# A hybrid decoder layer on one core: 18 output products of the second token tile move behind the last attention head, and the first feed-forward block is computed one token tile at a time

## The chip, the core and the metric

The kernel runs on one core of a Trainium2 chip. The metric is the device time of one execution in microseconds (us). The core has five engines that run their own instruction queues and meet only at semaphores: PE (TensorE, the matrix products; its weight loads are shown apart as PEld), DVE (VectorE), ACT (ScalarE), POOL (GpSimd) and SP, whose queue issues most of the DMAs here.

## The reference, cut to what matters

One layer on 256 tokens of width 1024, float32. `x` is projected; two groups of 8 heads (latent attention and block-sparse attention, which on 256 tokens is plain causal attention with a distance penalty) give `concat(A, B)` of width 1024. Then:

```
x = layer_norm(alpha * x + concat(A, B) @ W_o)
h = causal_depthwise_conv3(x @ W_up)          # 2 * 2816 columns
x = layer_norm(alpha * x + (silu(gate) * up) @ W_down)
```

The tolerance of float32 is reached by splitting each factor of a product into a rounded part (`hi`, float32r) and a remainder (`lo`): a product is hi x hi, hi x lo and lo x hi. TensorE takes a float32r product in one record; a plain float32 product (the scores and values of the heads) shows as two.

## The kernel before, in words

Tokens lie in two tiles of 128 (t = 0, 1), the model width in eight blocks of 128 (k = 0 to 7), the feed-forward width in 22 blocks (f = 0 to 21), each with a gate half (w = 0) and an up half (w = 1).

**Attention.** 16 heads run one behind the other: `scores` (PE), softmax (DVE and ACT), `transposes` (PE), `values` (PE). Between these steps the PE is given independent products out of the list `todo`, in pieces of so many moving rows as `FILL` says: 1500 after the scores, 1500 after the values, 1700 after the transposes. The list holds first the projections that later heads need and then the output products `wo` of block k and token tile t (`gen_wo`, 3 products for each of two groups of 512 columns). One product counts its moving columns, and a piece ends with the product that reaches the number. In this stage the PE's products are kept in the order of the program.

**Output products behind the last head.** What is left of the list runs, then, in this order: two runs of `late` (k = 4 and 5 of tile 1, first column group, 3 products each), the 6 products of (k = 7, t = 0), which end tile 0, and the six other runs of `late` (first column group of k = 6 and 7, then the second group of k = 4 to 7). The sums lie in PSUM tiles `pm`.

**First layer norm and turning.** Each step of it is pinned (`pin`, `tc.keep_in_program_order`), so that every engine takes these steps in the order of the program. Tile 0: add to the residual (L494), statistics (L500), aggregate (L505), root on ACT (L506), then the add of tile 1's first column group (L494), reciprocal (L511), shift (L515), scale on ACT (L528). PE turns tile 0 in two tiles of four 128x128 transposes, `a0` (k 0 to 3) and `a4` (k 4 to 7). Gain and offset (`affine`, L551 on ACT, L553 on DVE) write `x1T`; `high` (L557, ACT) writes `x1hi`, `low` (L560, POOL or DVE) writes `x1lo`. Tile 1 follows with four tiles of two transposes. `keep_warm` (L101) puts five idle products between.

```
ln_root(0, 0)
ln_add(0, 1, 0, r1, x_sb[:, 1, :], pm)
mu, rs, nm = ln_scale(0, 0)
ln_shift(mu, rs, nm)
```

**Feed-forward.** `up(f, w)` multiplies a block of `W_up` with `x1` (both token tiles): for f = 0 (and the very last half block) by 24 products of 256 columns (L611, L612, L615); for the others by 8 products of 512 columns (hi with x1hi and x1lo side by side, L621) and 8 of 256 (lo with x1hi, L624), whose two halves are then added by an ACT copy `hb` (L626) and a DVE add `h` (L628). These products are not pinned; the planner puts them where its own model finds room.

**Weights.** A block of weights is loaded into `raw`, cast to `hi` on ACT (L87), and `lo` is the difference on DVE (L88). Each of the three has 7 buffers. A block's `hi` and `lo` are free again when its last product is done. From f = 1 on, the splits of the up half and of f = 2 wait for the last steps of turning (`late_split`).

Of the kernel before, what the change touches and what calls it, by code (L numbers as in the profile page):

```python
# [33 lines left out]
TURN_AFTER = 4  # L34
LAG = 2
BEFORE = 2
A0, A4 = 2, 0
WARM = (6, 5)
WARM_NARROW = 3
HELD = 6  # L40
HALVES = ((0, 512), (512, 512))
COLS = ((HALVES, HALVES), (HALVES, ((0, 512), (512, 256), (768, 256))))
ATTW_BUFS = 2
FILL = (8000, 1500, 1500, 1700)
EARLY = 1
NARROW = 1
RES = 8
RAW_BUFS, HI_BUFS, LO_BUFS = 7, 7, 7

# [2 lines left out]
def layer_kernel(ctx: ExitStack, tc: tile.TileContext, a, out):  # L52
# [371 lines left out]
    todo = [("q1", gen_q(1), 0)] + [(f"va{t}", gen_va(t), 0) for t in range(NT)] + [("k2", gen_k(2), 0)]  # L424
    todo += [(f"q{pr}", gen_q(pr), 0) for pr in (2, 3)]
    todo += [(f"qk{w}{pr}", gen_qk(w, pr), 0) for pr in range(NP) for w in range(2)][EARLY:]
    todo += [(f"wo{k}{t}", gen_wo(k, t), 2 * k + 2) for k in range(NP) for t in range(NT)]
    todo += [(f"wo{k}0", gen_wo(k, 0), 2 * k + 2) for k in range(NP, KT - 1)]
    done = set()
    over = 0  # L430

# [18 lines left out]
    def run(gen):  # L450
        for _ in gen:
            pass
# [24 lines left out]
    x_sb = att_pool.tile([P, NT, D], F32, tag="m8b", name="x_sb")  # L477
    for t in range(NT):
        nc.gpsimd.dma_start(x_sb[:, t, :], a["x"][:, t, :])
    late = [(k, 1, (grp,)) for grp in COLS[0][1] for k in range(NP, KT)]  # L480
    for k, t, cols in late[:2] + [(KT - 1, 0, None)] + late[2:]:
        run(gen_wo(k, t, cols))

    r = acts.tile([P, NT, D], F32, tag="r", name="r")
    x1 = acts.tile([P, KT, 2, S], F32R, tag="x", name="x1")
# [5 lines left out]
    def ln_add(i, t, j, dst, res, acc):  # L491
        o, n = COLS[i][t][j]
        sl = slice(o, o + n)
        pin(nc.vector.scalar_tensor_tensor(dst[:, sl], res[:, sl], ALPHA, acc[t, o][:, :n], op0=ALU.mult, op1=ALU.add))  # L494

    def ln_part(i, t, j, src):
        w = min(n for _, n in COLS[i][t])
        o, n = COLS[i][t][j]
        for c in range(o // w, (o + n) // w):
            pin(nc.vector.bn_stats(lnst[:, i, t, c * 6:c * 6 + 6], src[:, c * w:(c + 1) * w]))  # L500
# [26 lines left out]
    for sl in halves:  # L527
        pin(nc.scalar.activation(r0[:, sl], r0[:, sl], AF.Identity, bias=nm, scale=rs))  # L528
    ln_part(0, 1, 0, r1)
    for j in range(1, len(COLS[0][1])):  # L530
        ln_add(0, 1, j, r1, x_sb[:, 1, :], pm)
        ln_part(0, 1, j, r1)

    class Turned:

# [10 lines left out]
        def affine(self, on_act, lo=0, hi=None):  # L546
            for i in range(self.n)[lo:hi]:
# [4 lines left out]
                else:  # L552
                    pin(nc.vector.tensor_scalar(dst, src, g1T[:, k:k + 1], b1T[:, k:k + 1],  # L553
                                                op0=ALU.mult, op1=ALU.add))

        def high(self):
            return pin(nc.scalar.copy(x1hi[:, self.ks, self.tk], self.x1T))  # L557

# [1 line left out]
            return pin(eng.tensor_tensor(x1lo[:, self.ks, self.tk], self.x1T,  # L560
                                         x1hi[:, self.ks, self.tk].bitcast(F32), op=ALU.subtract))

    a0, a4 = Turned(0, 0, 4, wk_tile), Turned(0, 4, 4, wk_tile)
    keep_warm(WARM[1], "warm1")
    a0.affine(True, 0, A0)
    ln_root(0, 1)
    a0.affine(True, A0)
    a0.high()
    a0.low(nc.gpsimd)
    a4.affine(False, 0, A4)  # L570
    mu, rs, nm = ln_scale(0, 1)
    for sl in halves:
        pin(nc.vector.tensor_scalar(r1[:, sl], r1[:, sl], mu, rs, op0=ALU.subtract, op1=ALU.mult))
    tiles = [Turned(1, k0, 2, wk_tile if k0 < 4 else acc_tile) for k0 in range(0, KT, 2)]
    a4.affine(False, A4)
    tiles[0].affine(True)
    tiles[0].high()
    a4.high()
    a4.low(nc.gpsimd)
    for i in range(1, 4):  # L580
        tiles[i].affine(False)
        tiles[i - 1].low(nc.vector)
        last_a = tiles[i].high()
    last_v = tiles[3].low(nc.vector)

    sm.__exit__(None, None, None)
    w2.__exit__(None, None, None)
# [14 lines left out]
            return split(raw, n, name)  # L602

    def up(f, w):
        raw = load(a["w_up"][f, :, w, :], CH, f"wu{f}{w}")
        hi, lo = late_split(raw, CH, f"wu{f}{w}", pin=1 <= f <= 2 and (f, w) != (1, 0))
        ph = wk_tile(f"ph{f}{w}")
        if f < NARROW or (f, w) == (NF - 1, 1):
            for k in range(KT):
                ks = slice(k * P, (k + 1) * P)  # L610
                nc.tensor.matmul(ph[:, :S], hi[:, ks], x1hi[:, k, :], start=(k == 0), stop=False)  # L611
                nc.tensor.matmul(ph[:, :S], lo[:, ks], x1hi[:, k, :], start=False, stop=False)  # L612
            for k in range(KT):
                ks = slice(k * P, (k + 1) * P)
                nc.tensor.matmul(ph[:, :S], hi[:, ks], x1lo[:, k, :], start=False, stop=(k == KT - 1))  # L615
            h = ph[:, :S]
        else:

            for k in range(KT):
                ks = slice(k * P, (k + 1) * P)  # L620
                nc.tensor.matmul(ph, hi[:, ks], x1[:, k].rearrange("p i t -> p (i t)"), start=(k == 0), stop=False)  # L621
            for k in range(KT):
                ks = slice(k * P, (k + 1) * P)
                nc.tensor.matmul(ph[:, :S], lo[:, ks], x1hi[:, k, :], start=False, stop=(k == KT - 1))  # L624
            hb = ff.tile([P, S], F32, tag=f"hb{w}", name=f"hb{f}{w}")
            nc.scalar.copy(hb, ph[:, S:])  # L626
            h = ff.tile([P, S], F32, tag=f"h{w}", name=f"h{f}{w}")
            nc.vector.tensor_tensor(h, ph[:, :S], hb, op=ALU.add)  # L628
        c = cw[:, w * NF + f, :]
        hc = ff.tile([P, S], F32, tag=f"hc{w}", name=f"hc{f}{w}")  # L630
        nc.scalar.activation(hc, h, AF.Identity, bias=c[:, 3:4], scale=c[:, 2:3])  # L631
        for j in (1, 2):
            nc.vector.scalar_tensor_tensor(hc[:, j:S], h[:, 0:S - j], c[:, 2 - j:3 - j], hc[:, j:S],  # L633
                                           op0=ALU.mult, op1=ALU.add)
        return hc
# [159 lines left out]
```

## Time and profile before

| | |
|---|---|
| median of three runs | 310.29 us (309.94 to 311.3) |
| profiled execution: its own time | 308.82 us |
| its span, first to last instruction | 307.0 us |
| PE busy | 296.1 us (96%) |
| PEld busy | 262.2 us (85%) |
| DVE busy | 237.3 us (77%) |
| ACT busy | 198.8 us (65%) |
| POOL busy | 31.4 us (10%) |
| mean granted TensorE clock | 0.994 |

The rows of the trace say what one engine did and what it waited for; times in them count from the span's start. The profiled execution took 1.5 us less than the median of the other runs, so that sums made on its trace are carried over to the median as differences.

### The profile page before, as it was taken

The numbers are of one execution on the slowest core, as the hardware profiler recorded it, in microseconds if no ns is written. First come the engines' busy times: TensorE is split into PE (matmuls) and PEld (weight loads), VectorE is DVE, ScalarE is ACT, GpSimd is POOL, SyncE is SP. The second block draws the span as 40 slices with busy tenths as digits, with TensorE's granted clock in tenths as the row PEclk, the third lists the DMA queues.
The fourth block names the chain that finished last, engine by engine and source line by source line (L and its number), as shares of the span: only waits on it lengthen the run. The fifth ranks groups of instructions, "written<-read, shape, count | busy, mean of one in ns | idle before, by whom it ended". The sixth has DMA issues, their size and how long they took to land.

```text
span 307.0 us, 4884 instructions
## 1 busy us (share of the span) xinstructions
PE 296.1 (96%) x1736; PEld 262.2 (85%) x1736; DVE 237.3 (77%) x475; ACT 198.8 (65%) x390; POOL 31.4 (10%) x43
## 2 busy tenths in 40 slices
PE   8999999999999989999999999999999999999990
PEld 7987999999888869888888888888888888888880
DVE  2878976656565387999999888888886978975595
ACT  4789996676655287977666657666676758634410
POOL 9430300035310021000000000000000000000030
PEclk9999999999999999999999999999999999999997
DMA  6998855273332104988865556555555776000003
GB/s 198 400 405 298 292 190 175 100 244 117 118 108 101 68 0 125 360 315 269 276 226 181 181 194 203 185 176 181 183 175 203 240 244 202 0 0 2 0 1 138
DMA packets 16216, 54.31 MB, mean 177 GB/s; under 512 B 1824, under 2 KB 2736, under 8 KB 16192
## 3 DMA queue, kind: packets, MB, share of 16 engines
q1 hardware_dynamic: 15840, 52.92, 49.7%
q0 software_dynamic: 352, 1.09, 1.2%
q8 instruction: 13, 0.21, 0.3%
q14 instruction: 11, 0.09, 0.1%
HBM read 52.95 MB, written 1.05 MB: 176 GB/s over the span
## 4 chain that ended last, share of the span: by engine, by line
PE 92%; DVE 3%; DMA 2%; ACT 1%; SPq 0%; issue 0%; DVEq 0%
PE ph L621 25%; PE pd L658 19%; PE ph L624 13%; PE pqk L279 7%; PE pm L279 7%; PE pv L247 4%; PE po L279 3%; PE pq L279 2%; PE sca L279 2%; DMA r_wc<-in_w_c 2%; PE scb L279 2%; PE pc L181 1%; PE ph L611 1%; PE ph L612 1%; PE ph L615 1%; PE pc L182 1%
## 5 line engine op out<-in xcount | busy, mean ns | idle before, releaser
L621 PE MATMUL ph<-x,h_wu 128*128 128x512 f32 x328 | 82.8, 393 | 0.0
L621 PEld LDWEIGHTS ph<-x,h_wu 128*128 128x128 f32 x328 | 59.1, 188 | 10.9
L88 DVE TENSOR_TENSOR l_wu<-r_wu,h_wu 128x1024 fp32r<-128x1024 f32 x44 | 53.5, 1219 | 7.7 <-ACT h_wu L87 7.3
L87 ACT CAST h_wu<-r_wu 128x1024 fp32r<-128x1024 f32 x44 | 45.8, 1048 | 6.2 <-PE ph L621 3.3
L633 DVE SCALAR_TENSOR_TENSOR hc<-h,cw,hc 128x255 f32<-128x255 f32 x82 | 39.3, 479 | 12.6 <-ACT hc L631 11.7
L624 PEld LDWEIGHTS ph<-x,l_wu 128*128 128x128 f32 x328 | 44.7, 190 | 3.4
L624 PE MATMUL ph<-x,l_wu 128*128 128x256 f32 x328 | 45.7, 282 | 0.0
L631 ACT ACTIVATE hc<-h,cw 128x256 f32<-128x256 f32 x41 | 24.6, 601 | 24.1 <-DVE h L628 24.1
L279 PE MATMUL pqk<-x,h_wqk 128*128 128x256 f32 x128 | 27.2, 298 | 0.0
L279 PEld LDWEIGHTS pqk<-x,h_wqk 128*128 128x128 f32 x128 | 20.6, 190 | 0.3
L88 DVE TENSOR_TENSOR l_wd<-r_wd,h_wd 128x1024 fp32r<-128x1024 f32 x16 | 19.5, 1220 | 0.9 <-ACT h_wd L87 0.9
L658 PE MATMUL pd<-l_wd,ghi 128*128 128x512 f32 (+1 forms) x80 | 20.1, 349 | 0.0
L658 PE MATMUL pd<-h_wd,glo 128*128 128x512 f32 (+1 forms) x80 | 20.1, 349 | 0.0
L658 PE MATMUL pd<-h_wd,ghi 128*128 128x512 f32 (+1 forms) x80 | 20.0, 348 | 0.0
L722 POOL TENSOR_TENSOR r<-r,lnv 128x512 f32<-128x512 f32 x1 | 1.3, 1293 | 180.8 <-ACT r L721 180.8
L279 PE MATMUL pqk<-x,l_wqk 128*128 128x256 f32 x64 | 19.1, 299 | 0.0
L628 DVE TENSOR_TENSOR h<-ph,hb 128x256 f32<-128x256 f32 x41 | 17.1, 417 | 2.0 <-ACT hb L626 2.0
L87 ACT CAST h_wd<-r_wd 128x1024 fp32r<-128x1024 f32 x16 | 16.7, 1045 | 2.8 <-PE ph L621 2.6
L645 ACT CAST ghi<-gt 128x256 fp32r<-128x256 f32 x22 | 8.9, 403 | 11.6 <-DVE gt L642 11.6
L658 PEld LDWEIGHTS pd<-h_wd,glo 128*128 128x128 f32 x80 | 14.0, 189 | 2.1
L658 PEld LDWEIGHTS pd<-l_wd,ghi 128*128 128x128 f32 x80 | 14.0, 189 | 2.1
L658 PEld LDWEIGHTS pd<-h_wd,ghi 128*128 128x128 f32 x80 | 14.0, 189 | 1.9
(166 smaller groups left out, 583.6 us busy)
## 6 DMA issues: line engine op xcount, KB each, us to landing
r_wu<-in_w_up SPq DMA_DIRECT2D x44, 512.0 KB, 3.7
r_wd<-in_w_down SPq DMA_DIRECT2D x22, 512.0 KB, 4.2
r_wqk<-in_w_qk SPq DMA_DIRECT2D x8, 512.0 KB, 5.1
r_wo<-in_w_o SPq DMA_DIRECT2D x8, 512.0 KB, 3.9
r_wv<-in_w_v SPq DMA_DIRECT2D x4, 512.0 KB, 7.7
lnv<-in_ln SPq DMA_DIRECT2D x4, 512.0 KB, 5.8
r_wc<-in_w_c SPq DMA_DIRECT2D x3, 416.0 KB, 6.6
r_wuq<-in_w_uq SPq DMA_DIRECT2D x2, 512.0 KB, 7.8
```

The costliest lines, as they stand in the source:

```text
L87: nc.scalar.copy(hi[:, c], raw[:, c])
L88: nc.vector.tensor_sub(lo[:, c], raw[:, c], hi[:, c].bitcast(F32))
L181: nc.tensor.matmul(pc[t][:, :NC0], xhi[:, k, tk], hi[:, o:o + NC0], start=(k == 0), stop=False)
L247: tc.keep_in_program_order(nc.tensor.matmul(pv[t], st[:, k, tk], mv[:, o:o + HALF], start=(k == 0 and i == 0), stop=(k == KT - 1 and i == 2)))
L279: ins = nc.tensor.matmul(*args, **kw)
L621: nc.tensor.matmul(ph, hi[:, ks], x1[:, k].rearrange("p i t -> p (i t)"), start=(k == 0), stop=False)
L624: nc.tensor.matmul(ph[:, :S], lo[:, ks], x1hi[:, k, :], start=False, stop=(k == KT - 1))
L628: nc.vector.tensor_tensor(h, ph[:, :S], hb, op=ALU.add)
L631: nc.scalar.activation(hc, h, AF.Identity, bias=c[:, 3:4], scale=c[:, 2:3])
L633: nc.vector.scalar_tensor_tensor(hc[:, j:S], h[:, 0:S - j], c[:, 2 - j:3 - j], hc[:, j:S], op0=ALU.mult, op1=ALU.add)
L645: rounded = nc.scalar.copy(ghi, gt)
L658: ins = nc.tensor.matmul(pd[t, o][:, :n], st[:, tk], mv[:, o:o + n], start=(f == 0 and i == 0), stop=(f == NF - 1 and i == 2))
```

## The change

Of the output products of tile 1 only those of k = 0 stay in the list; those of k = 1, 2 and 3 (3 blocks x 2 groups x 3 products = 18 products of 512 columns) are put at the head of `late`. The pieces of `FILL` shrink to 1250, 1250 and 1400. Behind the last head now run: the two groups of k = 1, the 6 products of (7, 0), eight runs (both groups of k = 2 and 3, first group of k = 4 to 7), the transposes of `a0`, one run, the transposes of `a4`, the last three runs. The five idle products are gone. The whole affine step of `a0` is on ACT, that of `a4` on DVE, and `a4.low` is on DVE. The second column group of tile 1 is added only behind that, and tile 1's layer norm follows.

The block f = 0 is computed per token tile: `first_high` is 8 products of 256 columns (W_up hi with x1hi and x1lo of one token tile), `first_low` 8 products of 128 columns (W_up lo with x1hi of one token tile). Both are pinned. Tile 0's are placed before and between the transposes of tile 1, tile 1's behind them, two blocks k at a time. The block f = 0 now also has the copy `hb` and the add `h`.

```diff
+KEPT = 1
+TURN = (8, 1)
-WARM = (6, 5)
+WARM = (6,)
-FILL = (8000, 1500, 1500, 1700)
+FILL = (8000, 1250, 1250, 1400)
-NARROW = 1
-    todo += [(f"wo{k}{t}", gen_wo(k, t), 2 * k + 2) for k in range(NP) for t in range(NT)]
-    todo += [(f"wo{k}0", gen_wo(k, 0), 2 * k + 2) for k in range(NP, KT - 1)]
+    todo += [(f"wo{k}{t}", gen_wo(k, t), 2 * k + 2) for k in range(KEPT) for t in range(NT)]
+    todo += [(f"wo{k}0", gen_wo(k, 0), 2 * k + 2) for k in range(KEPT, KT - 1)]
...
-    late = [(k, 1, (grp,)) for grp in COLS[0][1] for k in range(NP, KT)]
-    for k, t, cols in late[:2] + [(KT - 1, 0, None)] + late[2:]:
-        run(gen_wo(k, t, cols))
+    late = [(k, 1, (grp,)) for k in range(KEPT, NP) for grp in COLS[0][1]]
+    late += [(k, 1, (grp,)) for grp in COLS[0][1] for k in range(NP, KT)]
+
+    def late_rows(n):
+        for k, t, cols in late[:n]:
+            run(gen_wo(k, t, cols))
+        del late[:n]
+
+    late_rows(2)
+    run(gen_wo(KT - 1, 0))
+    late_rows(TURN[0])
...
     ln_part(0, 1, 0, r1)
-    for j in range(1, len(COLS[0][1])):
-        ln_add(0, 1, j, r1, x_sb[:, 1, :], pm)
-        ln_part(0, 1, j, r1)
...
+        def affine_high(self):
+            for i in range(self.n):
+                k = self.k0 + i
+                pin(nc.scalar.activation(x1hi[:, k, self.tk], self.ps[:, i * P:(i + 1) * P], AF.Identity,
+                                         bias=b1T[:, k:k + 1], scale=g1T[:, k:k + 1]))
...
-    a0, a4 = Turned(0, 0, 4, wk_tile), Turned(0, 4, 4, wk_tile)
-    keep_warm(WARM[1], "warm1")
-    a0.affine(True, 0, A0)
-    ln_root(0, 1)
-    a0.affine(True, A0)
+    a0 = Turned(0, 0, 4, wk_tile)
+    late_rows(TURN[1])
+    a4 = Turned(0, 4, 4, wk_tile)
+    late_rows(len(late))
+    a0.affine(True)
     a0.high()
     a0.low(nc.gpsimd)
-    a4.affine(False, 0, A4)
+    a4.affine(False)
+    a4.high()
+    a4.low(nc.vector)
+    for j in range(1, len(COLS[0][1])):
+        ln_add(0, 1, j, r1, x_sb[:, 1, :], pm)
+        ln_part(0, 1, j, r1)
+    ln_root(0, 1)
     mu, rs, nm = ln_scale(0, 1)
     for sl in halves:
         pin(nc.vector.tensor_scalar(r1[:, sl], r1[:, sl], mu, rs, op0=ALU.subtract, op1=ALU.mult))
...
+    def first_high(w, t, k0=0, n=KT):
+        tk = slice(t * P, (t + 1) * P)
+        o = ph_first[w].rearrange("p (i t) -> p i t", i=2)
+        for k in range(k0, k0 + n):
+            ks = slice(k * P, (k + 1) * P)
+            pin(nc.tensor.matmul(o[:, :, tk], w_first[w][0][:, ks], x1[:, k, :, tk], start=(k == 0), stop=False))
+
+    def first_low(w, t, k0=0, n=KT):
+        tk = slice(t * P, (t + 1) * P)
+        for k in range(k0, k0 + n):
+            ks = slice(k * P, (k + 1) * P)
+            pin(nc.tensor.matmul(ph_first[w][:, tk], w_first[w][1][:, ks], x1hi[:, k, tk], start=False, stop=(k == KT - 1)))
+
+    first_high(0, 0)
+    first_low(0, 0)
+    first_high(1, 0)
+    tiles = [Turned(1, k0, 2, acc_tile) for k0 in (0, 2)]
+    first_low(1, 0)
+    tiles += [Turned(1, k0, 2, acc_tile) for k0 in (4, 6)]
+    tiles[0].affine_high()
+    tiles[0].affine(False)
+    tiles[0].low(nc.vector)
+    tiles[1].affine(False)
+    tiles[2].affine(True)
+    tiles[1].high()
+    tiles[2].high()
+    tiles[3].affine(False)
+    for i in range(1, 3):
+        tiles[i].low(nc.vector)
+    last_a = tiles[3].high()
     last_v = tiles[3].low(nc.vector)
+    for k0 in range(0, KT, 2):
+        for part in (first_high, first_low):
+            for w in range(2):
+                part(w, 1, k0, 2)
```

## Rows read from the trace of the kernel before

**Rows 1.** Page: shares by engine, then the chain that ended last by engine.

```profile
PE 296.1 (96%) x1736; PEld 262.2 (85%) x1736; DVE 237.3 (77%) x475; ACT 198.8 (65%) x390; POOL 31.4 (10%) x43
...
PE 92%; DVE 3%; DMA 2%; ACT 1%; SPq 0%; issue 0%; DVEq 0%
```

**Rows 2.** Waits from 90 to 126 us: waiter <- releaser, us, times, longest.

```profile
DVE r L494 <- PE pm L279: 4.8, 2, 4.5
...
ACT h_wu L87 <- PE pm L279: 1.5, 2, 1.3
...
PEld ph L611 <- ACT x L557: 0.9, 1, 0.9
...
PEld x1t L544 <- ACT r L528: 0.8, 2, 0.5
...
PEld x1t L544 <- PE warm L101: 0.6, 1, 0.6
...
PEld po L279 <- ACT pTb L381: 0.2, 1, 0.2
```

**Rows 3.** Chain that ended last, 104 to 121 us: start, us, what.

```profile
103.88 5.62 PE pm L279 x24
...
115.39 0.23 PE ph L621
...
118.31 0.95 PE ph L615 x8
```

**Rows 4.** Timeline, PE and PEld, 104 to 128 us: start, us, instruction.

```profile
105.11 0.40 PE L279 MATMUL pm<-h_wo,aThi 128*128 128x512 f32 x1
...
109.53 0.42 PEld L544 LDWEIGHTS x1t<-ident,r 128*128 128x128 f32 x4 [0.49 <-ACT r L528]
...
110.62 1.20 PEld L101 LDWEIGHTS warm<-zero 128*128 128x128 f32 x10
...
120.54 1.55 PE L621 MATMUL ph<-x,h_wu 128*128 128x512 f32 x6
```

**Rows 5.** Timeline, DVE, 104 to 128 us.

```profile
107.72 0.64 DVE L494 SCALAR_TENSOR_TENSOR r<-x_sb,pm 128x512 f32<-128x512 f32 x1
...
108.28 0.15 DVE L511 RECIPROCAL lnst<-lnst 128x1 f32<-128x1 f32 x1
...
109.52 0.69 DVE L494 SCALAR_TENSOR_TENSOR r<-x_sb,pm 128x512 f32<-128x512 f32 x1 [0.28 <-PE pm L279]
...
112.66 2.00 DVE L553 TENSOR_SCALAR x1T<-x1t,vecs 128x128 f32<-128x128 f32 x6
...
120.00 1.23 DVE L88 TENSOR_TENSOR l_wu<-r_wu,h_wu 128x1024 fp32r<-128x1024 f32 x1 [2.03 <-ACT h_wu L87]
```

**Rows 6.** Timeline, ACT, POOL and again PE, 104 to 128 us.

```profile
108.67 1.52 ACT L528 ACTIVATE r<-r,lnst 128x512 f32<-128x512 f32 x2 [0.53 <-DVE lnst L515]
...
110.23 0.81 ACT L551 ACTIVATE x1T<-x1t,vecs 128x128 f32<-128x128 f32 x2
...
112.23 0.63 ACT L557 CAST x<-x1T 128x512 fp32r<-128x512 f32 x1
...
112.43 1.06 PE L544 MATMUL x1t<-ident,r 128*128 128x128 f32 x8 [0.42 <-DVE r L573]
...
112.94 1.27 POOL L560 TENSOR_TENSOR x<-x1T,x 128x512 fp32r<-128x512 f32 x1 [25.71 <-ACT x L557]
...
117.11 0.41 ACT L557 CAST x<-x1T 128x256 fp32r<-128x256 f32 x1 [1.03 <-DVE x1T L553]
```

**Rows 7.** Groups by shape, whole span: a DVE difference of 512 and of 256 columns.

```profile
L88 DVE TENSOR_TENSOR l_wv<-r_wv,h_wv 128x512 fp32r<-128x512 f32 x8 | 5.4, 689 | 2.1 <-ACT h_wv L87 2.1
...
L560 DVE TENSOR_TENSOR x<-x1T,x 128x256 fp32r<-128x256 f32 x4 | 2.1, 534 | 0.1
```

**Rows 8.** Timeline, PE, 0 to 10 us.

```profile
3.77 1.38 PE L101 MATMUL warm0n<-zero 128*128 128x64 f32 x6
```

**Rows 9.** Windows, last stretch: length, busy from PE to POOL, granted clock, DMA share, GB/s.

```profile
302.80:307.00 4.20, 0.00 (x0) 0.00 (x0) 1.04 (x3) 0.00 (x0) 0.00 (x0) 0.53 0.36 127
```

More of the change, by code (lines that the diff above doesn't have):

```diff
@@ L573, in layer_kernel @@
         pin(nc.vector.tensor_scalar(r1[:, sl], r1[:, sl], mu, rs, op0=ALU.subtract, op1=ALU.mult))
[L574 to L583, printed above, removed]
+    w_first = [load_split(a["w_up"][0, :, w, :], CH, f"wu0{w}") for w in range(2)]
+    ph_first = [wk_tile(f"ph0{w}") for w in range(2)]
+    def first_high(w, t, k0=0, n=KT):
[26 more added lines that the diff above has]
+    last_a = tiles[3].high()
     last_v = tiles[3].low(nc.vector)
+    for k0 in range(0, KT, 2):
+        for part in (first_high, first_low):
+            for w in range(2):
+                part(w, 1, k0, 2)
     sm.__exit__(None, None, None)
@@ L604, in up @@
     def up(f, w):
[L605 to L608, printed above, removed]
+        ph = ph_first[w] if f == 0 else wk_tile(f"ph{f}{w}")
+        if f:
+            raw = load(a["w_up"][f, :, w, :], CH, f"wu{f}{w}")
+            hi, lo = late_split(raw, CH, f"wu{f}{w}", pin=1 <= f <= 2 and (f, w) != (1, 0))
+        if (f, w) == (NF - 1, 1):
             for k in range(KT):
@@ L615, in up @@
                 nc.tensor.matmul(ph[:, :S], hi[:, ks], x1lo[:, k, :], start=False, stop=(k == KT - 1))
-            h = ph[:, :S]
-        else:
+        elif f:
             for k in range(KT):
@@ L624, in up @@
                 nc.tensor.matmul(ph[:, :S], lo[:, ks], x1hi[:, k, :], start=False, stop=(k == KT - 1))
+        if (f, w) == (NF - 1, 1):
+            h = ph[:, :S]
+        else:
             hb = ff.tile([P, S], F32, tag=f"hb{w}", name=f"hb{f}{w}")
```

## The prediction

> **What bounds the kernel now.** I began with the page's shares and its chain [rows 1]: PE is busy 96% of the span and holds 92% of the chain. So the kernel is the sum of its PE products plus the few places where PE has nothing to do, and a moved product gains only what it fills of those. The view of waits shows them between the last head and the feed-forward part [rows 2]: PE waits for ACT's scale of tile 0 (0.8 us in two waits), behind the idle products (0.6) and for the first x1 (0.9). Inside attention the only wait is 0.2 us, for the copy of the last head's turned weights.
>
> The chain gives prices: 24 products of 512 columns in 5.62 us, 0.234 each; 8 of 256 in 0.95, 0.119 each [rows 3]. Four transposes take 0.42 us [rows 4]. I measure the stretch from 105.11 (first product behind the end of tile 0's sum) to the first dense group of f = 1 at 120.54 [rows 4], less two f = 1 products that the planner slipped in at 0.23 each [rows 3]: to 120.07, so 14.96 us. Work in it: 18 x 0.234 = 4.21, 16 transposes 1.68, f = 0 as 48 x 0.119 = 5.71; together 11.60. **So 3.36 us are lost there**, and that is all that the change can win from this stage.
>
> **The 18 moved products.** They cost 4.21 us in attention and cost it again behind it; PE's sum is the same. In attention the chain of PE starts each step earlier. What that risks: the copy before the last values product is already late by 0.2 [rows 2], and the piece before it shrinks from 1700 to 1400 rows, from four products to three, so one product, 0.234, less cover. I put +0.2 us on it; the bounds are 0 (the copy comes earlier too) and 0.7 (a few heads more with such a wait). No DMA moves with the products. The hi and lo buffers of k = 1 to 3 do stay taken: seven blocks (k = 1 to 7) then fill all seven buffers, and the first three W_up splits, one of which already waits for these products in before [rows 2], come behind them. They are freed between 1.4 us before and 2.8 us after 105.11 on this clock, and first_high wants them at 117, so ACT's idle time hides them; DVE's three differences at 1.23 [rows 5] fall into its own wait, described next. If one lands on the chain instead, up to 1.2 us.
>
> **First stall, tile 0.** I keep the clock of before, with 105.11 as the common start, and take off the 4.21 at the end. Eight runs = 24 products end at 105.11 + 5.62 = 110.73. The first column group of tile 1 is complete only with the last of them: it starts at 110.50 and takes 0.40 [rows 4], so DVE can add it at 110.93. But that add stands, pinned, ahead of tile 0's reciprocal. Queued behind it on DVE are reciprocal, shift and statistics; ACT's scale waits for these, and the transposes of a0 for the scale. In before the same add ran at 107.72, the reciprocal at 108.28 [rows 5], the scale at 108.67 [rows 6], the transposes at 109.53 [rows 4]: 1.81 from add to transposes. So they come at 112.74. PE, free from 110.73, **waits 2.0 us**. The add cannot fall behind the reciprocal, since both are pinned.
>
> **Second stall, x1 of tile 0.** PE: a0 to 113.16, one run 0.70 to 113.86, a4 to 114.28, three runs 2.11 to 116.39. ACT's scale ends 0.95 + 1.52 after the add, 113.40; four affine steps at 0.81 a pair and the cast of 0.63 end at 115.7; POOL's difference takes 1.27 and starts 0.08 behind the cast [rows 6]: 117.1. DVE's four affine steps of a4 (six took 2.00 [rows 5], so 1.33) end at 115.85, ACT's cast at 116.5, DVE's difference of 512 columns (0.69 [rows 7]) at 117.2. first_high needs hi and lo, so it starts at 117.1: **0.7 us** lost.
>
> **The narrow products.** first_high costs like before, 32 x 0.119 = 3.81. The 32 products of 128 columns have no row in float32r. Bounds: by columns alone, the step from 256 to 512 (0.115 for 256) gives 0.063; if they run like a plain float32 product, which shows two records at 0.112 each (ten idle records: (1.20 - 0.19)/9 [rows 4]), 0.224. The rows nearest: records that also load 128x128 weights for 128 columns, 0.105 (four transposes in 0.42) to 0.112 [rows 4]. And at the start, on the lower clock, 64-column records followed each other at (1.38 - 0.40)/5 = 0.195 [rows 8], slower than their columns ask: the load of 128 weights seems to be the floor. On the full clock half of it, 0.098. I take 0.11: 3.52 us. So f = 0 costs 7.33 against 5.71, **+1.6 us**.
>
> The Trainium skill (TensorE: Matmul & The Clock Gate, Back-to-back issue gap) puts a sustained stream of pairs of weight load and 128-column product at about 81 ns. An estimate from that page would be 32 x 0.081 = 2.6 us, 0.9 less than by the rows; no run here shows such a stream in float32r.
>
> **Third and fourth stall, tile 1.** PE from 117.1: first_high to 118.05, first_low 0.88 to 118.93, the second first_high to 119.88. DVE, free at 117.2, adds the second column group of tile 1; in before such an add at 109.52 [rows 5] led to transposes at 112.43 [rows 6], 2.91 later: 120.1, PE waits 0.2. Transposes to 120.5, first_low to 121.4, transposes to 121.82. Tile 1's first x1 is ready at 121.8 (0.8 for the two affine steps, 0.42 to 0.53 for the difference [rows 7]). A group of two k costs 4 x (0.119 + 0.11) = 0.92, to 122.74. The next one waits: ACT takes the affine steps of the third tile first (to 122.67), then two casts of 0.41 [rows 6], DVE the affine steps of the fourth, then the difference: 123.65, **0.9 us**. Three more groups: 126.45. The planner can slip two f = 1 products in there, as it did before, 0.47: 125.97.
>
> **Sum.** 125.97 - 4.21 = 121.76 against 120.07, +1.7, and +0.2 from attention: **+1.9 us**. In losses: 3.4 go, about 3.3 come in other places, the narrow products add 1.6 and attention 0.2. The removed idle products cost nothing, they lay in the waits. The copy and add of f = 0 cost nothing as long as ACT and DVE keep their lead: before, the cast behind the last turning step ended its difference at 121.23 [rows 5], 3.7 after that last step (117.52 [rows 6]). Now the last step is at about 123.9, the difference at 127.6 plus up to 0.8 for copy and add, and PE wants it at 128.8. Without that cover, up to 1 us.
>
> The profiled execution took 308.82 (span 307.0 plus 1.8); it would take 310.7. The median of the runs is 310.29, so I forecast 310.29 + 1.9 = **312.2**. About 0.5%, 1.55 us, is what a measurement of this kernel can tell from no change.
>
> **Rivals.**
> - *Tile 0's chain is ready when PE comes.* If the reciprocal were not held behind the add, as in before, where it ran at 108.28, the transposes would start at 110.73, and everything behind moves up by 2.0: -0.1 us, 310.2, not slower. It decides from the point at which the first column group of tile 1 is summed by 108.3 on this clock. For it: 5.6 us of cover against a chain that took 4.4 (105.11 to 109.53). Against it: the pinned order.
> - *The moved products fill all that was lost.* -3.36 + 1.62 + 0.2: -1.5, 308.8. Against it: all of tile 1's chain still stands behind the last product.
> - *The narrow products run like float32*, 0.224 each. first_low's last three parts then set PE: transposes at 120.8, the second pair at 123.0, and the four groups at 1.37 each end at 129.4 instead of 126.45; less 0.23 for one slipped product: +4.9, with attention +5.1, 315.4. For it: no row shows otherwise.
> - *The clock falls, or f = 1 starves.* The granted clock fell to the lower level only in the last 4.2 us [rows 9], where PE has no product left; through the waits of [rows 2] it did not. If it fell in the new ones, the 3 to 5 us of products of f = 0 behind them would double; likewise up to +5.
>
> **How the numbers follow.** Chances: forecast with its stalls (+0.9 to +2.9) 0.45; tile 0's chain ready (-1.1 to +0.9) 0.20; all filled (below -1.1) 0.13; narrow as float32 (+2.9 to +5.5) 0.15; clock or starving 0.07. The range from -1.1 to +5.5 leaves out 0.13 below and about 0.04 above: **309.2 to 315.8**; the forecast's own range is 311.2 to 313.2. Slower by over 0.5%: 0.15 + 0.07 + two thirds of the forecast, 0.30, **0.52**. Same: the rest of it, 0.15, and nearly all of the first rival, 0.19, **0.34**. Faster: **0.14**.
>
> **What would show it.** Right: a wait of PE near 2 us before a0's transposes, released by ACT's scale, with DVE's add of tile 1 just ahead of the reciprocal; 0.7 before first_high, released by POOL; 0.2 and up to 0.9 around tile 1; first_low at 0.11 apart. Wrong: a0's transposes straight behind the eight runs; first_low at 0.06 or 0.22; waits of PE inside attention above 0.7 in sum; the granted clock below 1.00 before the end; PE waiting for l_wu at f = 1.

## The result and the profile after

The changed kernel took 313.52 us (median of 312.29, 312.36, 314.69 and 314.76) beside 310.12 us for the kernel before on the same chip: ratio 1.0109, 95% interval 1.0077 to 1.0142. Run again later (experiment 9, thirteen times) it took 312.56 us beside 310.13: ratio 1.0062, 1.0035 to 1.0088 (the two medians alone give 1.0078). The two intervals overlap from 1.0077 to 1.0088. So the change costs 1.9 to 3.4 us, by the overlap about 2.5. The forecast was 312.2, +1.9: slower, as foreseen, and a little too small.

On the traces the difference is larger, and it can be placed. One landmark before the change's work and one behind it stand in both kernels: the first scores product, and the first low group of f = 1. First the kernel before, then the changed one, PE timeline:

```profile
34.29 0.82 PE L279 MATMUL sca<-kT,qT 128*128 128x128 f32 x4
...
121.93 1.12 PE L624 MATMUL ph<-x,l_wu 128*128 128x256 f32 x8
```

```profile
34.74 0.82 PE L280 MATMUL sca<-kT,qT 128*128 128x128 f32 x4
...
101.87 0.40 PE L280 MATMUL pm<-h_wo,aThi 128*128 128x512 f32 x1
...
109.53 0.66 PE L550 MATMUL x1t<-ident,r 128*128 128x128 f32 x4 [1.89 <-ACT r L537]
...
113.81 1.29 PE L604 MATMUL ph<-x,h_wu 128*128 128x256 f32 x8 [0.40 <-POOL x L572]
114.94 1.01 PE L610 MATMUL ph<-x,l_wu 128*128 128x128 f32 x8
115.79 1.17 PE L604 MATMUL ph<-x,h_wu 128*128 128x256 f32 x8
117.04 0.65 PE L550 MATMUL x1t<-ident,r 128*128 128x128 f32 x4
...
119.69 0.71 PE L604 MATMUL ph<-x,h_wu 128*128 128x256 f32 x4 [0.69 <-ACT x1T L557]
...
121.21 0.74 PE L604 MATMUL ph<-x,h_wu 128*128 128x256 f32 x4
...
122.19 0.69 PE L604 MATMUL ph<-x,h_wu 128*128 128x256 f32 x4
...
123.11 0.69 PE L604 MATMUL ph<-x,h_wu 128*128 128x256 f32 x4
...
125.70 1.12 PE L673 MATMUL ph<-x,l_wu 128*128 128x256 f32 x8
```

From landmark to landmark: 87.64 us before, 90.96 after, **+3.32**. From there to the end of the span both take 185 (307.0 - 121.93 = 185.1, 310.6 - 125.70 = 184.9). On these two traces all of the loss is made between the first scores and f = 1. (Below, *net* times count from the first scores product, so that the 0.45 us by which the second execution started later drops out.) That times differ by 2.5 where traces differ by 3.3 is mostly the profiled execution of before: at 308.82 us it was quicker than all but one of the 35 runs of before beside experiments 9 to 12, and 1.3 us below their median, while the profiled execution of the changed kernel (312.36) lies only 0.2 below its own. What the execution of before escaped, its trace can't show.

The first product behind the sum of tile 0 starts at 101.87 instead of 105.11 [rows 4], net 3.69 earlier; 4.21 left attention, so attention gave back 0.52. The waits that answer to [rows 2], 84 to 128 us, columns as there:

```profile
ACT h_wu L88 <- PE pm L280: 7.1, 3, 5.0
...
PEld x1t L550 <- ACT r L537: 2.3, 1, 2.3
...
DVE x1T L559 <- ACT x L565: 0.9, 1, 0.9
PEld ph L604 <- ACT x1T L557: 0.9, 1, 0.9
PEld ph L604 <- POOL x L572: 0.8, 1, 0.8
PEld po L280 <- ACT pTb L382: 0.7, 2, 0.4
...
PEld ph L604 <- DVE x L572: 0.4, 1, 0.4
...
PEld x1t L550 <- DVE r L592: 0.3, 1, 0.3
```

The stall of 2 us before the transposes of a0 is there (2.3 for the weight load, 1.9 for the products), and so are 0.8 behind POOL and the small ones of tile 1. Two lines weren't foreseen: the 0.9 before the first x1 of tile 1, and DVE itself waiting for ACT's L565. The DVE timeline, which answers to [rows 5], and ACT's beside it:

```profile
101.75 1.23 DVE L89 TENSOR_TENSOR l_wu<-r_wu,h_wu 128x1024 fp32r<-128x1024 f32 x1 [5.61 <-ACT h_wu L88]
102.90 1.28 DVE L503 SCALAR_TENSOR_TENSOR r<-x_sb,pm 128x512 f32<-128x512 f32 x2
...
105.29 1.21 DVE L89 TENSOR_TENSOR l_wu<-r_wu,h_wu 128x1024 fp32r<-128x1024 f32 x1
106.41 0.20 DVE L514 BATCH_NORM_AGGREGATE lnst<-lnst 128x2 f32<-128x12 f32 x1
106.53 1.17 DVE L89 TENSOR_TENSOR l_wu<-r_wu,h_wu 128x1024 fp32r<-128x1024 f32 x1
107.67 0.69 DVE L503 SCALAR_TENSOR_TENSOR r<-x_sb,pm 128x512 f32<-128x512 f32 x1
108.28 0.16 DVE L520 RECIPROCAL lnst<-lnst 128x1 f32<-128x1 f32 x1
...
113.41 0.90 DVE L572 TENSOR_TENSOR x<-x1T,x 128x512 fp32r<-128x512 f32 x1 [0.69 <-ACT x L569]
...
118.36 0.73 DVE L559 TENSOR_SCALAR x1T<-x1t,vecs 128x128 f32<-128x128 f32 x2 [0.92 <-ACT x L565]
```

```profile
104.87 1.05 ACT L88 CAST h_wu<-r_wu 128x1024 fp32r<-128x1024 f32 x1 [0.35 <-PE pm L280]
105.94 1.28 ACT L515 ACT_TABLE_LOAD   x1
107.24 0.29 ACT L515 ACTIVATE lnst<-lnst,epsc 128x1 f32<-128x1 f32 x1
...
108.66 1.52 ACT L537 ACTIVATE r<-r,lnst 128x512 f32<-128x512 f32 x2 [1.13 <-DVE lnst L524]
```

This is where the lead of 3.69 us goes. The buffers for W_up come free late: ACT's three casts wait 7.1 us for PE's output products, 1.5 in the kernel before [rows 2]. So all three of W_up's differences now stand in tile 0's chain on DVE: one ahead of the first add (the add has a net lead of 2.63 over before), one ahead of the aggregate, one ahead of tile 1's add. At the reciprocal the net lead is 0.45 us (108.28 in both, [rows 5]). The first add of before, for comparison:

```profile
105.08 1.28 DVE L494 SCALAR_TENSOR_TENSOR r<-x_sb,pm 128x512 f32<-128x512 f32 x2 [4.53 <-PE pm L279]
```

ACT's table of the square root is loaded behind the third cast, too.

### The profile page after: what moved, and what is told of

It is laid out like the page before. It is cut to its first block, busy times and chain, and to the rows that moved or that the text cites. A ratio compares the mean times of both kernels' runs of the same rounds, so it can differ in the third digit from the quotient of the medians.

```text
span 310.6 us, 4907 instructions
## 1 busy us (share of the span) xinstructions
PE 297.6 (96%) x1742; PEld 262.9 (85%) x1742; DVE 238.7 (77%) x478; ACT 198.4 (64%) x393; POOL 27.3 (9%) x42
## 3 DMA queue, kind: packets, MB, share of 16 engines
HBM read 52.95 MB, written 1.05 MB: 174 GB/s over the span
## 4 chain that ended last, share of the span: by engine, by line
PE 87%; DVE 7%; DMA 2%; ACT 1%; issue 1%; SPq 0%; DVEq 0%
PE ph L670 24%; PE pd L710 18%; PE ph L673 13%; PE pqk L280 7%; PE pm L280 4%; PE po L280 4%; PE pv L248 4%; PE pq L280 2%; DMA r_wc<-in_w_c 2%; PE sca L280 2%; PE scb L280 2%; DVE r L503 1%; DVE x1T L559 1%; PE pc L182 1%; DVE lnst L509 1%
## 5 line engine op out<-in xcount | busy, mean ns | idle before, releaser
L685 DVE SCALAR_TENSOR_TENSOR hc<-h,cw,hc 128x255 f32<-128x255 f32 (+1 forms) x86 | 40.9, 479 | 12.0 <-ACT hc L683 11.3
L683 ACT ACTIVATE hc<-h,cw 128x256 f32<-128x256 f32 x43 | 25.7, 601 | 24.0 <-DVE h L680 24.0
L280 PE MATMUL pqk<-x,h_wqk 128*128 128x256 f32 x128 | 27.9, 301 | 0.0
L680 DVE TENSOR_TENSOR h<-ph,hb 128x256 f32<-128x256 f32 x43 | 17.8, 416 | 1.6 <-ACT hb L678 1.6
```

What stands on the lines that cost most here:

```text
L280: ins = nc.tensor.matmul(*args, **kw)
```

## The experiments

**1. Reciprocal ahead of tile 1's add** (in the changed kernel).

```diff
-    ln_add(0, 1, 0, r1, x_sb[:, 1, :], pm)
     mu, rs, nm = ln_scale(0, 0)
     ln_shift(mu, rs, nm)
+    ln_add(0, 1, 0, r1, x_sb[:, 1, :], pm)
```

> The changed kernel with one edit: reciprocal and shift of tile 0 stand ahead of the add of tile 1's first column group on DVE. Theory A (only the pinned order holds tile 0's chain back): PE's wait of 1.9 us before a0's transposes goes and everything behind moves up by 1.9 us, about 1.6 us slower than the kernel before instead of 3.4. Theory B (the W_up splits, which come late because their buffers are taken, stand on the same chain): the root is ready only at 107.5 and the third difference ends at 107.7 in the trace of after, so the reciprocal moves up only from 108.28 to 107.7, and the whole gains 0.5 to 0.6 us.

312.23 us, ratio 1.005 (1.0028 to 1.0072). DVE and PE timelines:

```profile
106.43 1.17 DVE L89 TENSOR_TENSOR l_wu<-r_wu,h_wu 128x1024 fp32r<-128x1024 f32 x1
107.52 0.16 DVE L520 RECIPROCAL lnst<-lnst 128x1 f32<-128x1 f32 x1
...
107.79 0.69 DVE L503 SCALAR_TENSOR_TENSOR r<-x_sb,pm 128x512 f32<-128x512 f32 x1
```

```profile
108.77 0.66 PE L550 MATMUL x1t<-ident,r 128*128 128x128 f32 x4 [1.24 <-ACT r L537]
...
294.26 0.73 PE L710 MATMUL pd<-hd,ghi 128*128 128x512 f32 x2 [0.41 <-ACT ghi L697]
```

The transposes come 0.65 us earlier (net), the low group of f = 1 by 0.66, not by 2.0: behind the add stood the third difference, and the reciprocal now starts right behind that. The last line is a wait of PE near the end, 0.4 us for the last gate. The first trace of the changed kernel doesn't have it, but its second has (experiment 9), so it is no sign that a gain is given back; the part on the prediction comes back to it.

**2. The 18 products moved, the first block as before.**

```diff
-FILL = (8000, 1500, 1500, 1700)
+FILL = (8000, 1250, 1250, 1400)
-    ... for k in range(NP) for t in range(NT)]
+    ... for k in range(1) for t in range(NT)]
...
+    late = [(k, 1, (grp,)) for k in range(1, NP) for grp in COLS[0][1]]
...
```

> The kernel before with only the 18 products moved behind the last head and the smaller pieces; f = 0 and the turning as before. Theory A (tile 1's chain behind the last product sets this stage, so more products ahead of it cover nothing new): the stage behind the last product is as long as before and attention's new waits are added, +0.5 us against the kernel before (0.2 to 1.0). Theory B (the moved products fill what was lost): -1 us or more.

312.01 us, ratio 1.006 (1.0027 to 1.0092). Net, the low group of f = 1 comes 0.49 us later than before. From there to the end this execution takes 3.05 us more than that of before; 1.66 of it is the same wait as above:

```profile
294.57 0.73 PE L659 MATMUL pd<-hd,ghi 128*128 128x512 f32 x2 [1.66 <-ACT ghi L646]
```

The move by itself gains nothing: a0's transposes come 0.29 us later than before (net), so the lead from the moved products is lost on DVE again. One execution can't say how much of the late wait recurs.

**3. The block turned tile by tile, no product moved** (`KEPT = 4`, `TURN = (2, 1)`, `FILL` as before).

> The changed kernel with the 18 products back in attention (pieces of 1500, 1500, 1700 rows; two runs ahead of a0's transposes, one behind, three behind a4's); f = 0 per token tile as in the change. Theory A (the move is worth nothing because tile 0's chain ends at the same time in both traces, transposes of a0 at 109.53 in each): about the same as the changed kernel, +2.8 to +3.4 us against the kernel before. Theory B (the move gives cover that the per-tile block needs): clearly slower than the changed kernel, by 2 us or more.

313.26 us, ratio 1.0101 (1.0074 to 1.0128). The low group of f = 1 comes 3.78 us later than before, 0.46 later than in the changed kernel; PE waits 2.9 us instead of 1.9 before a0's transposes. Its time can't be told from the changed kernel's. On the traces, then, the block tile by tile costs 3.78, the move alone 0.49, both together 3.32: the loss is that of the block and of the order that comes with it, and 4.21 us of moved work buy back 0.46 of it.

**4. Tile 1's first block turned twice**, so that ACT (L565) and DVE (L559) read two PSUM tiles.

```diff
-            self.x1T = ... bufs=KT // n, ...
+            self.x1T = ... bufs=KT // n + t, ...
...
     tiles = [Turned(1, k0, 2, acc_tile) for k0 in (0, 2)]
+    twin = Turned(1, 0, 2, acc_tile)
     first_low(1, 0)
-    tiles += [Turned(1, k0, 2, acc_tile) for k0 in (4, 6)]
-    tiles[0].affine_high()
+    tiles += [Turned(1, k0, 2, wk_tile) for k0 in (4, 6)]
+    twin.affine_high()
```

> The changed kernel with the first two blocks of tile 1 turned twice, into two PSUM tiles, so that ACT (high part) and DVE (affine step) each read their own. Theory A (DVE's wait of 0.9 us for ACT there comes from both reading one PSUM tile): DVE starts with the transposes, tile 1's first lo part is ready 0.8 us earlier, 0.5 to 0.8 us faster than the changed kernel. Theory B (DVE waits for ACT for another reason, or the stage is set by the casts and differences behind): the wait stays, or goes without a change of the time.

With the second tile, the last two tiles of tile 1 move to the other set of PSUM tiles, and `x1T` gets one buffer more. 312.25 us, ratio 1.0069 (1.0042 to 1.0096). DVE timeline:

```profile
116.72 1.00 DVE L592 TENSOR_SCALAR r<-r,lnst 128x512 f32<-128x512 f32 x2
117.80 0.73 DVE L559 TENSOR_SCALAR x1T<-x1t,vecs 128x128 f32<-128x128 f32 x2
```

DVE's wait of 0.92 for ACT is gone, so sharing the tile was its cause. From tile 1's transposes to its first group it takes 2.24 us instead of 2.65. Less than 0.92 is gained, because DVE's difference then waits for ACT's rounded part (0.54). In this profile the low group of f = 1 comes 0.74 us later than in the first profile of the changed kernel, not earlier: behind the 1.9 us wait before a0's transposes the granted clock was 0.50 from 109 to 112 us. The stretch from tile 1's transposes to its first group lies behind that, at 1.00; in experiment 8, without such a fall there, the second turning moves the low group up by 0.34.

**5. The low products of f = 0 in 16 of 256 columns instead of 32 of 128**, all behind tile 1's x1.

```diff
-    first_low(0, 0)
     first_high(1, 0)
-    first_low(1, 0)
...
-  ..., x1[:, k, :, tk], start=(k == 0), stop=False)
+  ..., x1[:, k, :, tk], start=(k == 0 and t == 0), stop=False)
...
-  nc.tensor.matmul(ph_first[w][:, tk], ..., x1hi[:, k, tk], ...)
+  nc.tensor.matmul(ph_first[w][:, :S], ..., x1hi[:, k, :], ...)
```

> The changed kernel with the 32 low products of f = 0, 128 columns wide and one token tile each, turned back into 16 products of 256 columns for both tiles, issued behind tile 1's x1. If the narrow products are paid on the path, as the prediction booked them (about +1.6 us), 16 issues at 0.11 us fewer give 1.6 to 1.8 us back: some 311.8 us. If the 16 that stood ahead of tile 1's transposes only filled a time in which PE waits for tile 1's rows in any case, PE now waits there about 1.8 us longer than the 1.4 us it waits in the changed kernel, and the time stays at 313.2 to 313.8 us.

314.99 us, ratio 1.016 (1.0123 to 1.0197): worse than either reading expected. PE timeline:

```profile
117.43 1.11 PE L550 MATMUL x1t<-ident,r 128*128 128x128 f32 x8 [0.95 <-DVE r L592]
120.08 1.19 PE L604 MATMUL ph<-x,h_wu 128*128 128x256 f32 x4 [1.54 <-DVE x L572]
```

The 16 low products of tile 0 mostly filled a time in which PE waits for tile 1: without them it waits 0.95 + 1.54 there. On the waits the trace decides for the second reading; the time fits neither. The clock fell, too: windows of this profile (length, busy of PE, PEld, DVE, ACT and POOL, granted clock, DMA share, GB/s):

```profile
100.00:106.00 6.00, 6.00 (x27) 4.82 (x27) 4.66 (x7) 3.63 (x4) 0.00 (x0) 1.00 0.24 87
106.00:112.00 6.00, 4.11 (x19) 3.10 (x18) 3.02 (x8) 4.74 (x9) 0.00 (x0) 0.82 0.54 175
...
116.00:126.00 10.00, 7.51 (x48) 6.87 (x47) 6.69 (x17) 6.24 (x13) 0.00 (x0) 0.83 0.20 66
```

The clock was 0.50 from 110 to 113 us, behind the wait before a0's transposes that the changed kernel has as well, and again from 121 to 123, behind the 1.54. A profile of the changed kernel with the first of these falls is that of experiment 9: against it tile 1's first group comes 0.33 us earlier here (net 85.77 against 86.10), for some 1.7 us of products fewer. Behind that group this kernel falls back: its low group of f = 1 is 0.95 us later than experiment 9's, and PE waits 1.1 us for the last gate (experiment 9: 0.5). So the extra time over the second reading is likely the second fall and the late wait; neither was tested by itself.

**6. A larger last piece in attention.**

```diff
-            fill(FILL[3])
+            fill(FILL[3] if i < 2 * H - 1 else 2560)
```

> The changed kernel with the last filling piece of attention raised from 1400 to 2560 rows, so that more output products stand between the transposes of the last two heads and their value products. If attention's loss (0.52 us where 0.2 was forecast) is PE waiting for the two copies of the last heads' turned weights, 0.36 us each, these waits go and the products behind head (7,0) start 0.5 to 0.7 us earlier; then the first low group of f = 1 comes that much earlier too, and the time is 312.8 to 313.0 us unless the chain of late w_down transfers takes it back. If the loss lies elsewhere in attention, nothing moves: 313.5 us.

312.59 us, ratio 1.007 (1.0039 to 1.0101). The two waits for the copies (0.7 in sum) are gone from the trace; a0's transposes come 0.37 and the low group of f = 1 0.38 us earlier, net. So they were most of attention's loss of 0.52; in the time it can't be seen. That holds for experiments 1, 4, 6 and 7 alike: their ratios overlap the changed kernel's later one (1.0035 to 1.0088), and what each edit bought is read from its trace.

**7. Eight products of zeros in the wait before a0's transposes** (`keep_warm(8, "warm1")` ahead of them).

> The changed kernel with eight products of zeros (128 columns, no reader) on PE inside its 1.9 us wait for tile 0's first normalised half. The changed kernel's four times stand in two pairs, 312.3 and 314.7 us. If the wait itself lets the granted clock fall in some executions (one profile showed 0.5 right behind it), the upper pair goes: all times near 312.3 us, and no row of half clock from 108 to 113 us. If the clock falls for another reason, the times spread as before, median between 312.3 and 314.7 us. The first transposes come no earlier in either case.

312.06 us (311.51 to 312.96), ratio 1.0061 (1.004 to 1.0081). It looked as if the upper pair of times had gone; experiment 9 is needed to read it.

**8. Four mends at once** in the changed kernel: experiments 1, 4 and 6, and the square root's table loaded behind the last head.

```diff
+        finish_pair.last = nc.scalar.copy(aThi[:, i, :], po[:, :S])
...
+    preload(AF.Sqrt, 0, after=finish_pair.last)
```

> The changed kernel with four mends at once: tile 0's reciprocal ahead of tile 1's add on DVE, tile 1's first block turned twice so that ACT and DVE read two PSUM tiles, the larger last filling piece in attention, and the Sqrt table of ACT loaded behind the last head's copy instead of behind the W_up casts. If the terms of the loss found so far add up, the first low group of f = 1 comes earlier than in the changed kernel by 0.66 (scale) + 0.38 (two tiles) + 0.5 (piece) + about 0.5 (table) = 2.0 us, which still leaves it 1.3 us behind the kernel before. If all of that reached the end, the time is 311.5 us; if the late chain of w_down transfers gives back 0.5 to 0.8 us as in the earlier run with the scale first, 312.0 to 312.3 us. A time below 310.0 us would show that the block itself gains.

311.64 us, ratio 1.0046 (1.0025 to 1.0067). The low group of f = 1 comes 1.39 us earlier than in the changed kernel, not 2.0: a0's transposes 1.05, which is experiments 1 and 6 together, and 0.34 behind them. The table bought nothing: the reciprocal still starts right behind the third difference.

**9. The changed kernel again.**

> The changed kernel once more, unchanged, for more of its times: the run with zero products in the 1.9 us wait had nine times from 311.5 to 313.0 us, the changed kernel only four, from 312.3 to 314.8 us. If the wait lets the granted clock fall in some executions, more times show the same two groups, some near 312.2 and some near 314.7 us, and the median lies at 313 to 314 us, 1 to 1.5 us above the run with the zero products. If the two high times were chance, the median is 312.1 to 312.4 us and the zero products bought nothing.

312.56 us; twelve of thirteen times lie from 311.87 to 312.97 us, one at 314.94, and that one was profiled. Its windows, columns as in experiment 5, and a line of its PE timeline:

```profile
6.00:14.00 8.00, 6.26 (x26) 5.50 (x25) 5.83 (x13) 5.38 (x13) 4.25 (x4) 0.79 1.01 380
...
100.00:110.00 10.00, 8.28 (x36) 6.34 (x34) 7.44 (x12) 5.42 (x6) 0.00 (x0) 1.00 0.34 111
110.00:114.00 4.00, 3.83 (x14) 3.30 (x15) 0.67 (x3) 2.95 (x7) 0.57 (x1) 0.57 0.32 117
```

```profile
296.92 0.74 PE L710 MATMUL pd<-hd,ghi 128*128 128x512 f32 x2 [0.51 <-ACT ghi L697]
```

Right behind the 1.9 us wait the granted clock (1.00 is 2.4 GHz) falls to the lower level, 1.2 GHz, for most of 4 us, and the low group of f = 1 comes 1.15 us later than in the first profile of the same kernel. So the fall exists. It isn't all that this execution lost: its first scores product starts 0.63 us later, the clock being 0.79 from 6 to 14 us, and behind f = 1 it loses 0.8 us more, 0.5 of it in the wait for the last gate. The median with the zero products is 0.5 us lower, and the two ratios are equal (1.0062 and 1.0061). Three high times of seventeen without, none of nine with them: too few to call it shown that the zeros prevent them, and the two other high executions weren't profiled. Neither expectation was met; the fall behind the wait is an occasional price, 1.15 us in this execution, and no part of the usual difference.

**10. The same with five products of zeros in the rest of the wait.**

> The kernel with four mends at once (scale first, two tiles, larger last piece, table of the square root early) plus five products of zeros in what is left of the wait for tile 0's first half, 1.2 us. If a fall of the clock in that wait is part of its time, the median comes down from 311.64 to about 311.2 us and the upper end from 312.7; if the 1.2 us wait is too short to matter, 311.6 us again.

310.72 us, ratio 1.0015 (0.9988 to 1.0041): not to be told from before, and 1.8 us below the changed kernel measured beside it (experiment 9). Eleven of its twelve times lie below all thirteen of experiment 9. What the change cost is bought back as far as the times can tell; a gain isn't there, and on the trace the low group of f = 1 still comes 1.94 us later than in the profiled execution of before. That the zeros won the 0.9 us against experiment 8 isn't shown: the two intervals overlap, and in both profiles the low group of f = 1 is in the same place (89.58 and 89.57 net). Experiment 8's profiled execution lost 1.0 us ahead of the first scores product, with a granted clock of 0.82 from 4 to 10 us; in this one it was 1.00.

**11. The kernel before without its five products of zeros** (the change takes these away too).

```diff
-    keep_warm(WARM[1], "warm1")
```

> The kernel before, without the five products of zeros that it issues between tile 0's and tile 1's transposes; the change takes these away too. Nothing else differs. They occupy PE in a wait from 110.7 to 112.4 us. If an unfilled wait of that length lets the clock fall in some executions, the median rises from 310.3 by 0.5 to 1.5 us and half clock shows near 112 us in some profile; if not, it stays at 310.3 us or falls by up to 0.2 us, since tile 1's first transposes waited 0.6 us for the zero products by the waits.

310.53 us, ratio 1.001 (0.9978 to 1.0042), 308.39 to 314.09. No difference that this measurement can tell, and the granted clock is 1.00 from 100 to 126 us in its profile; costing this at nothing was right within 0.4%.

**12. W_up's first three differences out of DVE's chain** (in the kernel of experiment 10): one behind tile 1's statistics, two on POOL; the third split's cast moves behind tile 0's last cast.

```diff
...
+        with tc.issue_after(first.ins):
+            eng.tensor_tensor(lo, raw, hi.bitcast(F32), op=ALU.subtract)
...
```

> The same as the kernel with the mends and the zero products, and the differences of the first three W_up splits taken out of DVE's chain for tile 0: one behind tile 1's first statistics, two on POOL, the third split's cast behind tile 0's last cast. In the changed kernel these three stand before, inside and behind tile 0's statistics. If they are what held tile 0's chain (first add 1.0 us late, aggregate 1.2 us late), tile 0's transposes come 1.0 to 1.2 us earlier than in the kernel with the mends, the wait before them goes, the first low group of f = 1 comes 0.6 to 1.0 us earlier, and the time is 310.3 to 311.0 us, level with the kernel before at best. If the two POOL differences slow DVE or come late for their products, nothing is gained: 311.2 to 312.0 us.

311.12 us, ratio 1.0015 (0.9988 to 1.0043): nothing gained over experiment 10. DVE, POOL and PE timelines:

```profile
100.57 1.29 DVE L504 SCALAR_TENSOR_TENSOR r<-x_sb,pm 128x512 f32<-128x512 f32 x2 [4.76 <-PE pm L280]
...
103.66 0.17 DVE L521 RECIPROCAL lnst<-lnst 128x1 f32<-128x1 f32 x1 [0.36 <-ACT lnst L516]
103.86 1.88 DVE L525 SCALAR_TENSOR_TENSOR lnst<-lnst 128x1 f32<-128x1 f32 x1
```

```profile
103.34 2.39 POOL L605 TENSOR_TENSOR l_wu<-r_wu,h_wu 128x1024 fp32r<-128x1024 f32 x1 [20.68 <-ACT h_wu L603]
```

```profile
106.21 1.28 PE L102 MATMUL warm<-zero 128*128 128x128 f32 x10
107.32 0.60 PE L552 MATMUL x1t<-ident,r 128*128 128x128 f32 x4
```

The reciprocal comes 3.73 us earlier than in the changed kernel (net 69.81 against 73.54). 1.04 of that experiment 10 has as well (net 72.50); the other 2.69 came with these differences taken away, so they were what held it. But a0's transposes come only 0.28 us earlier than in experiment 10, the low group of f = 1 0.23. The shift, one column that took 0.16 elsewhere, takes 1.88 and ends when POOL's difference does (105.74 and 105.73). The Trainium skill (SBUF — State Buffer, SBUF: two separate sides) says that DVE and POOL share a pair of ports under an exclusive lock, and that a POOL operation that reads SBUF and started first holds it to its end against a DVE operation with two inputs in SBUF; this row agrees. The reciprocal, with one input, took 0.17 us beside the same POOL operation. And PE, done at 106.2, runs the zero products to 107.3, although ACT's scale of the first half, begun at 105.78, is half through its 1.52 us at 106.5: in the changed kernel the transposes start 0.87 behind that scale (108.66 to 109.53), so an estimate from these rows is that the zeros held them by 0.67. The same kernel without the zeros, and with the POOL work elsewhere, was not tried.

## Why the prediction was right, and where it was off

The direction and most of the mechanism held: what was lost between heads and feed-forward isn't filled but moves, and the narrow products run at the price that was put on them. The size of the first stall came out right by luck, and one step, tile 1's chain, was wrong. By time the sum was +1.9 against +1.9 to +3.4, on the trace +1.9 against +3.3. On the clock of before, less the moved 4.21 and with the 0.2 of attention, its points can be laid beside the changed kernel's, less the 0.45 of its later start:

| point | forecast | measured | off |
|---|---|---|---|
| transposes of a0 | 108.73 | 109.08 | +0.35 |
| first_high | 113.09 | 113.36 | +0.27 |
| transposes of tile 1 | 116.09 | 116.59 | +0.50 |
| first group of tile 1 | 117.81 | 119.24 | +1.43 |
| next group | 119.64 | 120.76 | +1.12 |
| end of f = 0, less slipped products | 121.96 | 123.35 | +1.39 |

**Attention (0.2, bounds 0 to 0.7):** 0.52. PE's weight loads wait for three late copies instead of one: 0.7 for the last two heads' and 0.2 for an early head's (at 42.8 us). The sum of 0.9 is above the 0.7 that the prediction named as a sign of being wrong; what it cost is 0.52, inside the bounds. Experiment 6 took the 0.7 away.

**First stall (2.0):** 1.9, released by ACT's scale as said. But the reason was only half right. I held that the add waits for PE's products and that the three W_up differences fall into DVE's own wait. The trace shows the add starting right behind the third difference, at 107.67; PE's sum for it was complete at 107.64 (107.24 and 0.40), so either cause alone would have set the start of the add. Experiment 1 gained 0.65 and not the 2.0 of the rival *tile 0's chain is ready*, and experiment 12 shows that the differences held the chain. The bound "up to 1.2 us if one lands on the chain" was the true case, with three of them; that they end within 0.03 us of PE's sum is luck, and so is the right size of the stall.

**Second stall (0.7):** 0.8 (0.4 on the products), released by POOL, as said. DVE's difference beside it took 0.90, where I took 0.69 [rows 7]; with the 0.35 that a0's transposes were late, that is about what makes tile 1's transposes 0.50 late.

**Narrow products (0.11 each):** 8 in 0.85 (114.94 to 115.79), 0.106; a group of two k in 0.92 (122.19 to 123.11), as forecast. The rival *like float32* is out. The estimate of 0.081 from the Trainium skill (TensorE: Matmul & The Clock Gate, Back-to-back issue gap) is not reached in this stream; the measured spacing decides. One of the supports for 0.11 is weaker than it was put: [rows 8] were read as the lower clock, but the profile's granted clock there is 1.00; only the spacing of the 416-column products, 0.35 us up to 9.2 and 0.19 from 9.5 on, speaks for the lower level. (Two small sums are off, without effect: 0.063 should be 0.061 or 0.062, and 126.45 should be 126.40.) And "+1.6 us" is no price on the path: by experiment 5, half of these products lie for the most part in waits that stay when they go.

**Tile 1's chain:** the step that failed. I counted 1.7 us from its transposes to the first group; it took 2.65. In it DVE waits 0.92 until ACT has read the same PSUM tile, which the forecast let run side by side. Experiment 4 took that wait away and 0.41 of the 2.65; the second turning that it needs makes ACT's rounded part later. The Trainium skill (PSUM — Partial Sum Buffer, PSUM bank collisions raise a hardware error) says that two engines must not be in one PSUM bank and the same quadrant of 32 partitions at once, reads against reads included, and that the compiler orders them; the trace agrees on the order: DVE starts at 118.36, behind ACT's 0.81 us of reading, which began at 117.51. The next wait was 0.4 instead of 0.9, and the planner slipped in one product of f = 1, not two (0.24).

**The clock (0.07):** did fall behind the new wait in some executions (the profiles of experiments 4, 5 and 9), for less than the +5 I put on it (1.15 us up to f = 1 in experiment 9), and not in the median.

**The cover at f = 1:** held; PE waits for no W_up there. What was not foreseen is the end, 170 us later, where PE waits for the last gate in many of the traces: 0.3 to 0.5 us in experiments 1, 3, 4, 8, 9 and 12, 1.1 in 5, 1.7 in 2. It is no price of a lead: experiment 9, the changed kernel itself and late at f = 1, has it, and experiment 10, with a lead of 1.38 us, doesn't. It follows how long ACT's casts of the late w_down blocks wait for their transfers: where that is 4.2 to 5.1 us in sum PE doesn't wait, at 5.2 to 5.6 it waits 0.3 to 0.5, at 6.0 1.1, at 6.7 1.7. No run changed these transfers, so that they set the wait is argued, not shown.

## What to carry to other kernels

Before moving filler work to cover a latency chain, list everything that will stand in that chain's engine queues at the new time, unpinned work too: here weight splits that became ready late because the moved products held their buffers took 3.2 of 3.7 us of lead. Give two engines that should work side by side a PSUM tile each. And when one cause explains a stall, undo just that cause: if the stall shrinks by a third, a second one ends just behind it.

## What the runs showed of the hardware

- A difference of 1024 columns on POOL held a one-column operation of DVE for 1.7 us (1.88 instead of 0.16, experiment 12). A DVE difference of 512 columns took 0.88 to 0.90 where POOL's still ran for its first 0.3 us (the changed kernel: DVE from 113.41, POOL to 113.76), and 0.69 where POOL's was already done (experiment 4).
- The granted clock fell to its lower level behind the PE wait of 1.9 us before a0's transposes in the profiles of experiments 4, 5 and 9. The same wait left it at 1.00 in the first profile of the changed kernel and in experiment 6, and so did one of 2.85 us in experiment 3: the length of the wait alone doesn't decide it.
